# A streaming encoder layer on one core: where x's squares are summed, what TensorE does while x loads, and when three tensors are fetched

## The chip, the cores and the metric

The kernel runs on one core of one Trainium2 chip. The core has TensorE (PE, matrix products; its weight loads are listed as PEld), VectorE (DVE), ScalarE (ACT), GpSimd (POOL) and SyncE (SP, which here only issues DMAs). The metric is the device time of one execution in microseconds; lower is better. All data are fp32. A product of full precision is made of three fp32r products, of operands that were split into a high and a low part.

## What is computed

One layer for 512 prompt tokens and 128 sample tokens (640 in all, width 1024):

```python
x = x + 0.5 * swiglu(rms_norm(x, norm_ffn1_g), ffn1_w_in, ffn1_w_out)      # width 2816
h = rms_norm(x, norm_mix_g)
x = x + (g_ret * (retention(h) @ w_br_ret) + g_fox * (attention(h) @ w_br_fox)) @ w_out
x = x + 0.5 * swiglu(rms_norm(x, norm_ffn2_g), ffn2_w_in, ffn2_w_out)
x = x + (p @ w_ple) * sigmoid(rms_norm(x, norm_ple_g) @ w_ple_gate)        # p: the embedding, width 256
```

`rms_norm` divides each token by the root of the mean of its squares and multiplies by a gain for each of the 1024 channels. The mixer's states and caches are outputs too.

## The kernel before, in words

x is kept transposed: 8 chunks of 128 channels, each 128 x 640 tokens. The gain is multiplied in when a chunk is split into its high part (ACT) and low part (DVE). The divisor of each token is a factor of a product's columns, so the products can start before it is known; it is `rb` (broadcast over the partitions) or `rtok` (by token).

**The start.** SP issues x in four groups of 256 channels, and between them the weights of the first two of 22 units of 128 channels of the first feed-forward (`first_raw`). In `x_in(q)` PE transposes the group's chunks, DVE and ACT copy them out of PSUM (L644, L645), and they are split (L348 and L340 on ACT, L349 and L341 on DVE). `plain[0].products(ops, j)` multiplies the group by unit 0's weights, which `split_w` has split (L269 ACT, L270 DVE) in pieces of four chunks. `x_out(q)` writes the chunk to DRAM and calls `add_square`: ACT squares it (L511), and PE sums the squares of each token by products with a column of ones (L513, into a PSUM bank `sizes`). After the last group `token_root` works out the inverse roots in ten small DVE steps (L326 to L333), copies them to `rtok` (L518), `row_stats` broadcasts them by PE, ACT copies them out (L529), and `act` can scale unit 0's result (L546 on DVE, `Silu` L547 on ACT, L548). Three units are computed so (`Plain`). Eight 2 KB PSUM banks are shared: six named `pa`, two named `pg`. `plain[0]` holds four of `pa`, so only the first half of `plain[1]` can run before L546.

**The units after.** From unit 3 (f = 3) on, a unit is a `Seven`: seven products in place of eight, of sums of quarters of the weights (three sums in `first`, L403 to L405) and sums of x's parts (`sums`, L357 to L361, split by L291 and L292). `ffn` runs the units in groups of 8, 8 and 6, and after each group a projection adds to x's chunks, which SP fetches from DRAM and, but for the last group of the second feed-forward, writes back. In that last projection `done` is `to_ple`, which hands each chunk to the third norm.

**The second feed-forward's start.** Unit 0's weights are loaded during the mixer's last product (`begun`); then the last two quarters of the embedding's product (`w_ple`) are computed in `pg` banks and written to DRAM (`ple`, L1431), and `ffn` loads unit 1's weights (`up_raw`, L535). Two buffers hold raw weights.

**The last stage.** For each quarter q of the channels and each token block t, PE multiplies by the gate's weights, `out(t)` fetches the embedding's rows from `ple`, takes the sigmoid (L1637), multiplies (L1638), adds x, transposed back by PE (L1642), and writes the result (L1643).

**Order.** A planner gives each engine an order from a simulated timeline, and each engine keeps to its order, DMA issues on SP included. `after` and `load` add edges to that order: `load(out, in, lead)` keeps a DMA behind a PE instruction some microseconds earlier, so that no buffer is taken too soon. `blk` has 38 buffers of 128 x 640, `att` and `tmp` have 8 each.

Of the kernel before, what the change touches and what calls it, by code (L numbers as in the profile page):

```python
# [19 lines left out]
P = 128  # L20
# [111 lines left out]
def kernel(  # L132
# [101 lines left out]

    def load_gains(n0, gs):
        rows = tmp([P, P])[:len(gs) * KC, :]
        for n, g in enumerate(gs):
            nc.scalar.dma_start(rows[n * KC:(n + 1) * KC, :], g[0].rearrange("(c p) -> c p", p=P))
        gb, at = bank("pg"), slice(n0, n0 + len(gs))
        transpose(gb[:, :len(gs) * KC], rows)  # L240
        nc.vector.tensor_copy(gains[:, at].rearrange("p n c -> p (n c)"), gb[:, :len(gs) * KC])
        nc.vector.tensor_scalar(less[:, at], gains[:, at], -1.0, None, op0=ALU.mult)

    load_gains(0, (norm_ffn1_g,))


# [104 lines left out]

    def sums(ops, x0, x1, g0, g1, less, later=None):


        b12, d13, d24 = tmp(), att(shape=(P, 2, H2)), att(shape=(P, 2, H2))
        x21, x22 = (x1[:, sl] for sl in HALVES)
        nc.scalar.activation(b12, x0[:, H2:], AF.Copy, scale=g0)  # L357
        nc.vector.scalar_tensor_tensor(d13[:, 0, :], x0[:, :H2], g0, b12, op0=ALU.mult, op1=ALU.subtract)
        nc.vector.scalar_tensor_tensor(d24[:, 0, :], x22, g1, d13[:, 0, :], op0=ALU.mult, op1=ALU.add)
        nc.vector.scalar_tensor_tensor(d13[:, 1, :], x22, less, b12, op0=ALU.mult, op1=ALU.add)  # L360
        nc.vector.scalar_tensor_tensor(d24[:, 1, :], x21, g1, d24[:, 0, :], op0=ALU.mult, op1=ALU.subtract)  # L361
        if later:
# [27 lines left out]
    class Seven:  # L390
# [7 lines left out]

        def first(self, spare=False):

            a11, a12, a21, a22 = self.given
            self.as_is = Parts().add(a11, spare), Parts().add(a22, spare)
            nc.vector.tensor_tensor(a11, a21, a11, op=ALU.add)  # L403
            nc.vector.tensor_tensor(a21, a21, a22, op=ALU.add)
            nc.vector.tensor_tensor(a22, a11, a22, op=ALU.add)  # L405
            return self
# [51 lines left out]
    class Norm:  # L458
# [22 lines left out]

        def add_sums(self, c, x0, x1, later=None):
            sums(self.ops, x0, x1, self.gain(c), self.gain(c + 1), less[:, self.n, c + 1:c + 2], later)

# [22 lines left out]

        def add_square(self, ps, xc, first, last):

            sq = att(shape=(P, T))  # L510
            nc.scalar.activation(sq, xc, AF.Square)  # L511
            for t in range(TB):
                mm(ps[:, t:t + 1], sq[:, t * P:(t + 1) * P], ones[:, 0:1], first and t == 0, last, skip_group_check=True)  # L513

        def token_root(self, ps):
            rt = rsqrt_mean(ps[:, :TB], TB, 1.0 / D)
            self.rtok = const.tile([P, TB], F32, name=nm("rtok"))
            nc.vector.tensor_copy(self.rtok, rt)  # L518

# [17 lines left out]

    def ffn(xd, norm, w_in, w_o, done, ahead=None, begun=None):
        pair0 = 0
        for npair in F_GROUPS:  # L540
# [19 lines left out]
            for f in fs:  # L560
# [16 lines left out]
                if f != fs[-1]:  # L577
                    q = Seven(*quarters(up_raw(w_in, f + 1))).split()
                while waiting and f > 0:
# [37 lines left out]

    def first_raw(f, u):
        cols = slice(u * DFF + f * P, u * DFF + (f + 1) * P)
        nc.sync.dma_start(raws[f][:, 8 * u:8 * u + 8, :], w_in[:, cols].rearrange("(c p) n -> p c n", p=P))  # L620

    with tc.manual_schedule(engines={mybir.EngineType.SP}):
        for q in range(KC // 2):
            cols = slice(q * 256, (q + 1) * 256)
            xi = big((P, TB, 256))
            nc.sync.dma_start(xi[:, :4, :], x_prompt[0, :, cols].rearrange("(t p) d -> p t d", p=P))
            nc.sync.dma_start(xi[:, 4, :], x_sample.rearrange("b l d -> (b l) d")[:, cols])
            xins.append(xi)
            if q < 2:
                first_raw(0, q)  # L630
        first_raw(1, 0)
        first_raw(1, 1)
        nc.sync.dma_start(sm[:, P:], c_small[:, P:])
    norm1 = Norm(0)
    xs0 = []
    sizes = bank("pg")

    def x_in(q):
        for c in (2 * q, 2 * q + 1):
            xc = blk()  # L640
            b, b2 = bank(), bank("pg")
            for t in range(TB):
                transpose(b[:, t * P:(t + 1) * P] if t < 4 else b2[:, :P], xins[q][:, t, c % 2 * P:(c % 2 + 1) * P])
            nc.vector.tensor_copy(xc[:, :S], b)  # L644
            nc.scalar.copy(xc[:, S:], b2[:, :P])  # L645
            xs0.append(xc)
            norm1.add_parts(c, xc)
            if c % 2 == 0:
                first_parts(norm1.ops, xc[:, H2:], norm1.gain(c), "b12")

    def x_out(q):
        for c in (2 * q, 2 * q + 1):
            nc.sync.dma_start(xd[0][c], xs0[c])
            norm1.add_square(sizes, xs0[c], c == 0, c == KC - 1)

    plain = [Plain(raws[0])]
    for j in range(KC // 2):
        x_in(j)
        plain[0].products(norm1.ops, j)
        if j:  # L660
            x_out(j - 1)
        if j == 2:
            load_gains(1, (norm_mix_g, norm_ffn2_g, norm_ple_g))
    x_out(3)
    norm1.token_root(sizes)
    b0, b1 = bank("pg"), bank("pg")
    norm1.row_stats([b0, b1[:, :P]])

    def step(n):
        def run(act):  # L670
# [4 lines left out]
            for j in ((0, 1), (2, 3), ())[n]:  # L675
                norm1.add_sums(2 * j, xs0[2 * j], xs0[2 * j + 1])
            act(plain[n])
# [937 lines left out]

    x = []

    def to_ple(xc):
        x.append(xc)
        norm3.add(xc)  # L1620
        norm3.square(xc)

    ffn(xd[1], norm2, ffn2_w_in[0], ffn2_w_out[0], to_ple, begun=begun)

# [3 lines left out]
    for q in range(4):  # L1628
# [59 lines left out]
```

## Time and profile before

| | before |
|---|---|
| three runs | 1669.32, 1670.46, 1672.25 us; median 1670.46 |
| the profiled execution | 1668.46 us |
| its span, first to last instruction | 1666.4 us |
| PE busy | 1648.0 us (99%) |
| DVE, ACT busy | 1172.2 us (70%), 743.6 us (45%) |
| DMA | 248.67 MB, mean 149 GB/s |

The span is the stretch that the trace covers; the device time adds some 2 us around it. A matmul's record is longer than its share of PE's time, since records overlap; the pace is read from the starts, or from the chain of waits, whose pieces do not overlap. An fp32 matmul leaves two records.

### The profile page before, as it was taken

What the parts mean: (1) busy time and instruction counts of PE and PEld (TensorE: products, weight loads), DVE (VectorE), ACT (ScalarE), POOL (GpSimd) and SP (SyncE); (2) the same over time, 40 slices, a digit from 0 to 9 for tenths busy, and PEclk for the clock granted to TensorE, in tenths of its full rate; (3) what the DMA queues carried; (4) which work ended last, traced back from release to release, by engine and by line L of the source; (5) the groups of instructions that cost most, each with busy time, mean ns of one, the idle gap of its engine ahead of it and who ended that gap; (6) DMA issues with size and microseconds to landing.
All of it is one profiled execution on the core that took longest, in us unless ns stands there. A gap on an engine that the chain in (4) does not pass through costs nothing.

```text
span 1666.4 us, 30484 instructions
## 1 busy us (share of the span) xinstructions
PE 1648.0 (99%) x12073; PEld 1575.3 (95%) x12073; DVE 1172.2 (70%) x2524; ACT 743.6 (45%) x1506; POOL 1.4 (0%) x6
## 2 busy tenths in 40 slices
PE   8999999999999999999999999999999999999998
PEld 7999999999999888888789888999999999999998
DVE  5985687577787746667688876657885688568663
ACT  5652354244455545444434455435653355235432
POOL 0000000000000000000000000000000000000000
PEclk9999999999999999999999999999999999999999
DMA  7144324433533234576775687634324423432332
GB/s 242 52 133 140 108 78 139 146 94 106 176 111 109 70 115 148 218 259 243 284 235 168 219 272 260 228 108 146 105 78 171 132 77 120 145 116 87 122 125 87
DMA packets 228303, 248.67 MB, mean 149 GB/s; under 512 B 15264, under 2 KB 195392, under 8 KB 224064
## 3 DMA queue, kind: packets, MB, share of 16 engines
q1 hardware_dynamic: 227952, 246.64, 45.5%
q8 instruction: 95, 1.56, 0.4%
q14 instruction: 48, 0.39, 0.1%
q10 hardware_dynamic: 208, 0.08, 0.0%
HBM read 198.04 MB, written 48.65 MB: 148 GB/s over the span
## 4 chain that ended last, share of the span: by engine, by line
PE 96%; DMA 3%; DVE 1%; ACT 0%; issue 0%; SPq 0%; DVEq 0%; ACTq 0%
PE pa L205 73%; PE pg L205 19%; PE pa L228 4%; DMA raw<-in_ffn_w_in_dram 1%; DMA kv<-zdram 1%; DMA out_dram<-kv 0%; DMA zdram<-blk 0%; DMA tmp<-ple 0%; PE pg L228 0%; ACT wh L269 0%; DVE wl L270 0%; DVE tmp L1642 0%; ACT tmp L1637 0%; DVE kv L1397 0%; DVE tmp L1638 0%
## 5 line engine op out<-in xcount | busy, mean ns | idle before, releaser
L269 ACT CAST wh<-raw 128x512 fp32r<-128x512 f32 (+1 forms) x525 | 316.0, 613 | 489.8 <-PE pa L205 291.8
L205 PE MATMUL pa<-blk,wh 128*128 128x320 f32 x2344 | 512.2, 311 | 3.8 <-ACT blk L348 1.2
L270 DVE TENSOR_TENSOR wl<-raw,wh 128x512 fp32r<-128x512 f32 (+1 forms) x525 | 351.4, 678 | 93.3 <-ACT wh L269 88.3
L205 PEld LDWEIGHTS pa<-blk,wh 128*128 128x128 f32 x2344 | 388.0, 189 | 11.9 <-issue 2.8
L205 PE MATMUL pa<-blk,wl 128*128 128x320 f32 x1172 | 343.9, 309 | 0.0
L205 PE MATMUL pa<-kv,wh 128*128 128x320 f32 x1344 | 251.4, 308 | 0.0
L205 PEld LDWEIGHTS pa<-blk,wl 128*128 128x128 f32 x1172 | 216.0, 188 | 0.0
L205 PEld LDWEIGHTS pa<-kv,wh 128*128 128x128 f32 x1344 | 210.7, 188 | 0.0
L205 PE MATMUL pg<-blk,wh 128*128 128x320 f32 x768 | 176.8, 316 | 2.0 <-DVE blk L788 1.9
L205 PE MATMUL pa<-blk,blk 128*128 128x320 f32 (+2 forms) x1064 | 167.1, 304 | 0.0
L205 PE MATMUL pa<-kv,wl 128*128 128x320 f32 x672 | 155.2, 308 | 0.0
L205 PE MATMUL pg<-wh,blk 128*128 128x256 f32 x784 | 152.9, 289 | 1.6 <-ACT tmp L1430 1.6
L205 PEld LDWEIGHTS pa<-blk,blk 128*128 128x128 f32 (+1 forms) x1064 | 151.4, 183 | 2.0 <-PE pa L205 1.2
L205 PEld LDWEIGHTS pg<-blk,wh 128*128 128x128 f32 x768 | 127.5, 188 | 8.8 <-issue 4.5
L205 PEld LDWEIGHTS pg<-wh,blk 128*128 128x128 f32 x784 | 123.4, 189 | 6.2 <-issue 3.0
L205 PE MATMUL pg<-blk,wl 128*128 128x320 f32 x384 | 118.9, 310 | 0.0
L205 PE MATMUL pg<-wl,blk 128*128 128x256 f32 x392 | 112.9, 289 | 0.0
L205 PEld LDWEIGHTS pa<-kv,wl 128*128 128x128 f32 x672 | 112.8, 188 | 0.0
L270 DVE TENSOR_TENSOR blk<-raw,blk 128x512 fp32r<-128x512 f32 x82 | 56.4, 688 | 54.7 <-ACT blk L269 33.6
L269 ACT CAST blk<-raw 128x512 fp32r<-128x512 f32 x82 | 50.6, 621 | 80.1 <-DMA raw<-in_ffn_w_in_dram 63.3
L205 PE MATMUL pa<-wh,blk 128*128 128x256 f32 (+1 forms) x416 | 78.9, 285 | 0.0
L205 PEld LDWEIGHTS pg<-wl,blk 128*128 128x128 f32 x392 | 73.9, 189 | 2.5 <-issue 1.7
(260 smaller groups left out, 2175.1 us busy)
## 6 DMA issues: line engine op xcount, KB each, us to landing
raw<-in_ffn_w_in_dram SPq DMA_DIRECT2D x88, 512.0 KB, 5.2
raw<-in_w_in_mix_dram SPq DMA_DIRECT2D x25, 1024.0 KB, 5.7
raw<-in_ffn_w_out_dram SPq DMA_DIRECT2D x16, 1024.0 KB, 5.2
kv<-in_cache_fox_k_dram SPq DMA_DIRECT2D x16, 1024.0 KB, 7.0
kv<-in_cache_fox_v_dram SPq DMA_DIRECT2D x16, 1024.0 KB, 8.4
xd<-blk SPq DMA_DIRECT2D x48, 320.0 KB, 2.6
blk<-xd SPq DMA_DIRECT2D x48, 320.0 KB, 5.4
zdram<-blk SPq DMA_DIRECT2D x32, 320.0 KB, 2.8
```

The lines of the kernel that those rows point to most:

```text
L205: i = nc.tensor.matmul(out, lhsT, rhs, start=start, stop=stop, **kw)
L228: tick(nc.tensor.transpose(out, in_, ident[: in_.shape[0], : in_.shape[0]]), 0.11)
L269: nc.scalar.copy(hi, src)
L270: nc.vector.tensor_tensor(lo, src, hi, op=ALU.subtract)
```

## The change

x's squares are summed over channels on ACT, from the rows of x as they were loaded (tokens on partitions): one `Square` with a sum for each token block and group, 20 in all, then one DVE reduction; the products with ones and the bank `sizes` go. Each square is placed behind a PE instruction, and the `sums` of x's parts are placed behind the root. PE gets nine 128 x 128 fp32 matmuls of ones before x is there, and two on the first chunk. The gains' rows are loaded at the start, into `att` buffers. The first group of x and unit 0's first half of weights are loaded in two pieces each. In each `Seven` after another, the first sum of the weights is placed behind the three sums of the unit ahead. Unit 1 of the second feed-forward is loaded before the embedding's last products, which alternate between `pa` and `pg` banks. The rows of `ple` are fetched in the last projection, three loads for each quarter, into `blk` buffers, in place of 20 loads in the last stage.

```diff
+    def keep_busy(times, x=None):
+        for _ in range(times):
+            nc.tensor.matmul(busy[:, :P], ones, ones if x is None else x[:, :P], start=True, stop=True)
+
+    keep_busy(9)
+    flip_gains(0, 1, load_gains((norm_ffn1_g,)))
+    more = load_gains((norm_mix_g, norm_ffn2_g, norm_ple_g))
...
-    def sums(ops, x0, x1, g0, g1, less, later=None):
+    def sums(ops, x0, x1, g0, g1, less, later=None, behind=None):
...
-        nc.scalar.activation(b12, x0[:, H2:], AF.Copy, scale=g0)
+        i = nc.scalar.activation(b12, x0[:, H2:], AF.Copy, scale=g0)
+        if behind:
+            after(i, behind, "the tokens' sizes go first")
...
-        def first(self, spare=False):
+        def first(self, spare=False, behind=None):
...
-            nc.vector.tensor_tensor(a11, a21, a11, op=ALU.add)
+            i = nc.vector.tensor_tensor(a11, a21, a11, op=ALU.add)
+            if behind:
+                after(i, behind, "the sums of the block ahead go first")
...
-        def add_square(self, ps, xc, first, last):
-            sq = att(shape=(P, T))
-            nc.scalar.activation(sq, xc, AF.Square)
+        def add_square(self, rows, behind):
+            if not self.squares:
+                self.by_rows = tiny(KC // 2 * TB)
             for t in range(TB):
-                mm(ps[:, t:t + 1], sq[:, t * P:(t + 1) * P], ones[:, 0:1], first and t == 0, last, skip_group_check=True)
+                at, sq = len(self.squares) * TB + t, tmp([P, 256])
+                i = nc.scalar.activation(sq, rows[:, t, :], AF.Square, accum_out=self.by_rows[:, at:at + 1])
+                after(i, behind, "the parts of x go first")
+            self.squares.append(rows)
+
+        def row_root(self):
+            total = tiny(TB)
+            nc.vector.tensor_reduce(total, self.by_rows[:, :len(self.squares) * TB].rearrange("p (q t) -> p t q", t=TB), axis=AX.X, op=ALU.add)
+            self.token_root(total)
...
                 if f != fs[-1]:
-                    q = Seven(*quarters(up_raw(w_in, f + 1))).split()
+                    ahead_of = q
+                    q = Seven(*quarters(second if second is not None else up_raw(w_in, f + 1)))
+                    q.first(True, ahead_of.summed).split()
+                    second = None
...
-            nc.sync.dma_start(xi[:, :4, :], x_prompt[0, :, cols].rearrange("(t p) d -> p t d", p=P))
-            nc.sync.dma_start(xi[:, 4, :], x_sample.rearrange("b l d -> (b l) d")[:, cols])
+            n = P if q == 0 else 256
+            for lo in range(0, 256, n):
+                nc.sync.dma_start(xi[:, :4, lo:lo + n], x_prompt[0, :, q * 256 + lo:q * 256 + lo + n].rearrange("(t p) d -> p t d", p=P))
+                if lo == 0:
+                    nc.sync.dma_start(xi[:, 4, :], x_sample.rearrange("b l d -> (b l) d")[:, cols])
+                if q == 0:
+                    first_raw(0, 0, 2 if lo else 0, KC if lo else 2)
             xins.append(xi)
-            if q < 2:
-                first_raw(0, q)
+            if q == 1:
+                first_raw(0, 1)
...
+            if c == 0:
+                keep_busy(2, xc)
...
-            norm1.add_square(sizes, xs0[c], c == 0, c == KC - 1)
+        norm1.add_square(xins[q], marks[max(q - 1, 0)])
...
         plain[0].products(norm1.ops, j)
+        marks.append(issued[-1][1])
...
-            load_gains(1, (norm_mix_g, norm_ffn2_g, norm_ple_g))
+            flip_gains(1, 3, more)
     x_out(3)
-    norm1.token_root(sizes)
+    norm1.row_root()
...
-                norm1.add_sums(2 * j, xs0[2 * j], xs0[2 * j + 1])
+                norm1.add_sums(2 * j, xs0[2 * j], xs0[2 * j + 1], behind=norm1.rooted)
...
+    second = up_raw(ffn2_w_in[0], 1)
     for q in range(2):
         for t in range(TB):
-            ps = bank("pg")
+            ps = bank("pa" if t % 2 else "pg")
...
     def to_ple(xc):
+        if len(x) % 2 == 0:
+            q, three = len(x) // 2, [blk([P, 2, 256]) for _ in range(3)]
+            for i, e in enumerate(three):
+                n = min(2, TB - 2 * i)
+                load(e[:, :n, :], ple[q, :, 2 * i:2 * i + n, :], 2.0)
+            embedding.append([three[t // 2][:, t % 2, :] for t in range(TB)])
...
-            pl, g = tmp([P, 256]), tmp([P, 256])
-            load(pl, ple[q, :, t, :])
+            g = tmp([P, 256])
             nc.scalar.activation(g, pss[t][:, :256], AF.Sigmoid, scale=norm3.rtok[:, t:t + 1])
-            nc.vector.tensor_tensor(g, g, pl, op=ALU.mult)
+            nc.vector.tensor_tensor(g, g, embedding[q][t], op=ALU.mult)
```

## Rows read from the trace of the kernel before

**Rows 1.** The page: the span, and each engine's busy time, share and instructions.

```profile
span 1666.4 us, 30484 instructions
PE 1648.0 (99%) x12073; PEld 1575.3 (95%) x12073; DVE 1172.2 (70%) x2524; ACT 743.6 (45%) x1506; POOL 1.4 (0%) x6
```

**Rows 2.** The waits of PE, whole span: who for whom, total, times, longest.

```profile
PE pa L228 <- DMA kv<-in_x_prompt_dram: 5.1, 1, 5.1
...
PE pg L228 <- DVE tmp L1642: 1.4, 1, 1.4
PE pa L205 <- ACT blk L348: 1.2, 1, 1.2
PE pa L205 <- DVE tmp L546: 1.0, 1, 1.0
...
PE pa L205 <- ACT wh L269: 0.8, 1, 0.8
```

**Rows 3.** The chain of waits, 0 to 52 us: start, us, what.

```profile
7.37 1.14 ACT wh L269 x2
...
9.02 0.64 PE pa L205
...
12.64 2.50 PE pa L205 x8
15.15 0.97 PE pa L228 x8
16.11 1.01 PE pg L205 x10
17.12 1.28 PE pa L205 x8
...
39.85 1.01 PE pg L205 x10
40.86 5.22 PE pa L205 x35
46.08 0.91 PE pg L205 x8
...
47.01 0.59 ACT blk L529
```

**Rows 4.** Groups of lines, 0 to 50 us: busy us, mean ns, idle before.

```profile
L205 PE MATMUL pg<-ones,att 128*128 128x1 f32 x80 | 9.7, 235 | 0.0
...
L511 ACT ACTIVATE att<-blk 128x640 f32<-128x640 f32 x8 | 5.8, 728 | 0.0
...
L358 DVE SCALAR_TENSOR_TENSOR att<-blk,gains,tmp 128x320 f32<-128x320 f32 x2 | 1.1, 543 | 0.0
```

**Rows 5.** The timeline of ACT in the mixing stage, 996 to 999 us.

```profile
997.40 0.43 ACT L1327 ACTIVATE tmp<-tmp 128x256 f32<-128x256 f32 x1
...
997.81 0.37 ACT L1430 COPY tmp<-pa 128x256 f32<-128x256 f32 x1
```

**Rows 6.** The timeline of DVE: the root's last step.

```profile
44.91 0.17 DVE L518 COPY rtok<-ty 128x5 f32<-128x5 f32 x1
```

**Rows 7.** The timeline of ACT, 66 to 70 us.

```profile
67.63 2.18 ACT L269 CAST wh<-raw 128x512 fp32r<-128x512 f32 x4 [4.20 <-DVE raw L405]
```

**Rows 8.** A stretch: busy us of PE, PEld, DVE, ACT, POOL; clock, DMA.

```profile
47.60:68.20 20.60, 20.03 (x137) 20.03 (x138) 20.18 (x38) 13.22 (x26) 0.00 (x0) 1.00 0.19 52
```

**Rows 9.** The same view, 10 to 15 us; the granted clock stands third from the end.

```profile
10.00:15.00 5.00, 4.98 (x17) 4.01 (x18) 3.01 (x5) 3.49 (x7) 0.00 (x0) 1.00 1.11 339
```

**Rows 10.** The chain of waits over the whole span.

```profile
48.17 424.45 PE pa L205 x2926
...
1172.66 4.44 DMA raw<-in_ffn_w_in_dram
...
1619.16 5.53 DMA tmp<-ple
```

**Rows 11.** The timeline of SP, 1565 us to the end: DMA issues.

```profile
1596.07 19.55 SPq L214 DMA_DIRECT2D tmp<-ple  x6
```

More of the change, by code (lines that the diff above doesn't have):

```diff
@@ L233, with load_gains, flip_gains @@
     less = const.tile([P, 4, KC], F32, name="less")
-    def load_gains(n0, gs):
-        rows = tmp([P, P])[:len(gs) * KC, :]
+    def load_gains(gs):
+        rows = att(shape=(P, P))[:len(gs) * KC, :]
         for n, g in enumerate(gs):
             nc.scalar.dma_start(rows[n * KC:(n + 1) * KC, :], g[0].rearrange("(c p) -> c p", p=P))
-        gb, at = bank("pg"), slice(n0, n0 + len(gs))
-        transpose(gb[:, :len(gs) * KC], rows)
-        nc.vector.tensor_copy(gains[:, at].rearrange("p n c -> p (n c)"), gb[:, :len(gs) * KC])
-        nc.vector.tensor_scalar(less[:, at], gains[:, at], -1.0, None, op0=ALU.mult)
-    load_gains(0, (norm_ffn1_g,))
+        return rows
+    def flip_gains(n0, n, rows):
+        gb, at = bank("pg"), slice(n0, n0 + n)
+        transpose(gb[:, :n * KC], rows)
+        nc.vector.tensor_copy(gains[:, at].rearrange("p n c -> p (n c)"), gb[:, :n * KC])
+        nc.vector.tensor_scalar(less[:, at], gains[:, at], -1.0, None, op0=ALU.mult)
+    busy = bank("pg")
+    def keep_busy(times, x=None):
[4 more added lines that the diff above has]
+    more = load_gains((norm_mix_g, norm_ffn2_g, norm_ple_g))
     def raw_unit(src, kc, n):
@@ L397, in __init__ @@
             self.given, self.w, self.banks = (a11, a12, a21, a22), [], {}
-        def first(self, spare=False):
+        def first(self, spare=False, behind=None):
             a11, a12, a21, a22 = self.given
             self.as_is = Parts().add(a11, spare), Parts().add(a22, spare)
-            nc.vector.tensor_tensor(a11, a21, a11, op=ALU.add)
+            i = nc.vector.tensor_tensor(a11, a21, a11, op=ALU.add)
+            if behind:
+                after(i, behind, "the sums of the block ahead go first")
             nc.vector.tensor_tensor(a21, a21, a22, op=ALU.add)
-            nc.vector.tensor_tensor(a22, a11, a22, op=ALU.add)
+            self.summed = nc.vector.tensor_tensor(a22, a11, a22, op=ALU.add).ins.name
             return self
@@ L480, in add_parts, with add_sums @@
                 first_parts(self.ops, xc[:, :H2], self.gain(c), "b11")
-        def add_sums(self, c, x0, x1, later=None):
-            sums(self.ops, x0, x1, self.gain(c), self.gain(c + 1), less[:, self.n, c + 1:c + 2], later)
+        def add_sums(self, c, x0, x1, later=None, behind=None):
+            sums(self.ops, x0, x1, self.gain(c), self.gain(c + 1), less[:, self.n, c + 1:c + 2], later, behind)
         def add_pair(self, x0, x1):
@@ L517, in token_root @@
             self.rtok = const.tile([P, TB], F32, name=nm("rtok"))
-            nc.vector.tensor_copy(self.rtok, rt)
+            self.rooted = nc.vector.tensor_copy(self.rtok, rt).ins.name
         def row_stats(self, dsts):
@@ L536, in up_raw, with ffn @@
         return r
-    def ffn(xd, norm, w_in, w_o, done, ahead=None, begun=None):
+    def ffn(xd, norm, w_in, w_o, done, ahead=None, begun=None, second=None):
         pair0 = 0
@@ L616, with first_raw @@
     raws = [raw_tile()[:, :16 * P].rearrange("p (c n) -> p c n", c=16) for _ in range(2)]
-    def first_raw(f, u):
+    def first_raw(f, u, lo=0, hi=KC):
         cols = slice(u * DFF + f * P, u * DFF + (f + 1) * P)
-        nc.sync.dma_start(raws[f][:, 8 * u:8 * u + 8, :], w_in[:, cols].rearrange("(c p) n -> p c n", p=P))
+        nc.sync.dma_start(raws[f][:, 8 * u + lo:8 * u + hi, :], w_in[lo * P:hi * P, cols].rearrange("(c p) n -> p c n", p=P))
     with tc.manual_schedule(engines={mybir.EngineType.SP}):
@@ L635 @@
     xs0 = []
-    sizes = bank("pg")
     def x_in(q):
@@ L653, in x_out @@
             nc.sync.dma_start(xd[0][c], xs0[c])
-            norm1.add_square(sizes, xs0[c], c == 0, c == KC - 1)
-    plain = [Plain(raws[0])]
+        norm1.add_square(xins[q], marks[max(q - 1, 0)])
+    plain, marks = [Plain(raws[0])], []
     for j in range(KC // 2):
@@ L1614 @@
     norm3 = Norm(3)
-    x = []
+    x, embedding = [], []
     def to_ple(xc):
+        if len(x) % 2 == 0:
[4 more added lines that the diff above has]
+            embedding.append([three[t // 2][:, t % 2, :] for t in range(TB)])
         x.append(xc)
@@ L1621, in to_ple @@
         norm3.square(xc)
-    ffn(xd[1], norm2, ffn2_w_in[0], ffn2_w_out[0], to_ple, begun=begun)
+    ffn(xd[1], norm2, ffn2_w_in[0], ffn2_w_out[0], to_ple, begun=begun, second=second)
     xs = norm3.xs
```

## The prediction, made before the change was run

> **What bounds the kernel now.** The page comes first: TensorE (PE) is busy 1648.0 of 1666.4 us, every other engine has room [rows 1]. So a microsecond counts only if PE stops executing something or stops waiting. The waits of PE come next: 5.1 us for the first piece of x, 1.2 us for ACT's first scaled part (L348), 1.0 us for DVE at L546, 0.8 us for an ACT cast at the start of the second feed-forward, 1.4 us for DVE at L1642 in the last stage [rows 2]; the rest lie in the mixing stage and inside the second feed-forward, which the change leaves alone. Then the chain of waits over the first 52 us [rows 3]. The reader is to see three things in it.
>
> First, the weights' cast ends the wait for data at 7.37, and the first product starts at 9.02. Second, the same 128x320 product is slow at first: 8 take 2.50 us from 12.64 (0.31 us each), 8 take 1.28 us from 17.12 (0.16 us each). [...] PE had done only transposes, then nothing, before 9.02, and products with gaps after it. Third, from 16.11 to 40.86 the chain holds 14 pieces of `pg L205`, from 1.01 to 0.12 us, in sum 7.45 us (first and last in [rows 3]): the products with ones that sum x's squares, 80 records in the groups of lines [rows 4].
>
> After 40.86 the chain runs through PE doing the first half of `plain[1]` while DVE works out the root, up to L518 at 44.91 [rows 6], 4.2 us with that step. Then `row_stats` at 46.08, ACT's copy at 47.01, DVE's L546, and PE goes on at 48.17. From there the chain stays on PE for 424.45 us [rows 10], so what is gained by the 48th microsecond is kept, if DVE follows: DVE is busy 20.18 of the 20.60 us from 47.60 to 68.20 [rows 8], and ACT's cast for the first `Seven` unit (f = 3) at 67.63 had waited 4.20 us for DVE's L405 [rows 7]. PE reaches f = 3 at about 48.17 + 144 x 0.149 = 69.6 (48 products of `plain[1]`, 96 of `plain[2]`, at 5.22/35 us). The weight is ready at about 68.3. So DVE is there with some 1 us to spare.
>
> **Squares on ACT.** PE loses 40 matmuls (80 records): 7.45 us off the chain. ACT loses 8 squares, 5.8 us [rows 4], and gets 20 of 128x256 with a sum. The nearest row is L1327, of the same shape and kind: it starts at 997.40, and the next instruction at 997.81 [rows 5], so 0.41 us each, 8.2 us in all; ACT pays 2.4 us more, and has that room if the squares fall into its gaps. Squares of group 3 may begin when `products(2)` are done. With the terms below PE finishes `plain[1]`'s first half near 37; 72 products (10.7 us) earlier is 26. Add 5 x 0.41, one reduction, and the root: 4.2 us as now [rows 3, 6], about half of that if no casts lie between its steps. `rtok` is ready at 31 to 33. Then `row_stats` 0.91, ACT 0.59 and L546's 0.5 us, about 33 to 35 [rows 3]: before PE is out of work. So the stall that ends at 48.17 (1.2 us after 46.98) goes as well. Cover: 2 to 4 us; without it PE waits.
>
> **Sums behind the root.** Their first eight DVE steps (0.543 us each by their row [rows 4], 4.3 us) now run before the root and will run after it. DVE then needs 20.6 + 4.3 = 24.9 us from the root to f = 3: 31 to 33 becomes 56 to 58. PE gets there at 37.8 + 21.5 = 59. Cost 0, cover 1 to 3 us, at most 4.3 us if it is used up. The other order put on DVE, the three sums of one `Seven` behind those of the unit ahead, is taken at 0: PE has no wait there now.
>
> **Products of ones while x loads.** Nine fp32 matmuls need only `ones`, which the first instruction of DVE sets. `row_stats` prices them: 0.114 us a record, two records each, double at the low level: 9 x 0.46 = 4.1 us, inside the 5.1 us wait [rows 2]. The two on x's first chunk lie inside the 1.2 us wait. Cost 0; an overrun of a few tenths is hidden too, since the first product waits for the weight. Gain: from 9.02 to 15.15 the chain did 16 products, worth 2.6 us at the high level, and a few transposes, about 1 us (8 take 0.97). At most 2.5 us can come back; not all, because the second half of the weights and x's next piece are still on their way. I take 1.5 and keep 0 to 2.5.
>
> [...]
>
> **Finer first loads.** Transposes of chunk 0 can start after half the bytes of x. But the first weight cast takes four chunks, and the pieces cut it after two, so it still waits for the same bytes, and SP issues two loads more. What remains is that ACT can do L348 before the casts: 9.02 becomes 8 at best, 9.3 if the extra issues delay the weight. 0.2 us gained; ends +1.1 and -0.3.
>
> **f = 1 of the second feed-forward loaded earlier.** Now its load is issued at 1172.66, behind writes of the embedding on SP, and is 4.44 us of the chain [rows 10]; ACT stands on it, and PE waits 0.8 us [rows 2]. Ahead of those writes it has the room left by the embedding weight's cast. Gain 0.8 (0 to 0.8); next late is nothing in that row. Alternate PSUM banks there: 0, no wait of PE is recorded.
>
> **Embedding fetched in the last projection.** The chain's `tmp<-ple` at 1619.16 lasts 5.53 us [rows 10] and ends in PE's wait of 1.4 us. 20 loads become 12 on SP, earlier. They lie behind PE work if they get their `blk` places. Gain 1.4 (0 to 1.4).
>
> **Sum.** 7.45 + 1.2 + 1.5 + 0.2 = 10.35 at the start, 0.8, 1.4: 12.55. The profiled execution took 1668.46 (span 1666.4), 2.0 below the median of the three runs, 1670.46. Against its own time the sum gives 1655.9; with the same 2.0, a median of 1657.9. The best ends (2.5, 1.1) give 1656.0, and an end for PE's small waits that this change doesn't name, some 2 us, 1653.5 or so.
>
> **The rivals.**
> *Root late, chance 0.15.* ACT keeps order: suppose parts and casts push the last square to 37. Then the root is ready near 41, L546 ends near 43.5 (4.7 us gained), and DVE's 24.9 us end near 66 (3.7 us gained at f = 3). 3.7 + 2.2 gives 1664.6. For it: ACT is in order and gets 2.4 us more. Against: over the span it is busy only 45% [rows 1], and the squares need nothing but x.
> *Clock not raised, chance 0.13.* The change does not do what it says there: the low pace lasts until 15 us as now [rows 3]; 12.55 - 1.5 = 11.05 gained, 1659.4. For it: the products thin out again while data arrive. Against: PE is then at work from 1 us on and not from 5. [...]
> *Root no earlier, sums behind it, chance 0.07.* If `rtok` came at 44.9 as now, 24.9 us end at 69.8, as now: the PE time freed turns into waits. Only the two late stalls are gained, at most 2.2 us: 1668 to 1671, no change.
> *Slower, chance 0.05.* The last projection. SP is in order, and today it stands 19.55 us on six `tmp<-ple` loads until `tmp` comes free [rows 11], with nothing urgent behind. The twelve new loads stand ahead of loads of x's chunks. Their places: 8 chunks + 16 parts + 1 + 12 = 37 of 38 `blk`. If a load stands like that, PE runs on for some two chunks (2 x 36 x 0.149 = 10.7 us) and then loses about 9 us. From the second such stand it outweighs the rest: 1657.9 + 18 = 1676. Against: the places of the second norm's operands come free just before.
>
> **How the numbers follow.** The forecast, 1658, has chance 0.60. Range 1653.5 to 1666: from the best ends to a little beyond the late root; it leaves out the last two rivals, 0.12, and a little of the edges. About 0.2% (3.3 us) can be told from no change: faster 0.60 + 0.15 + 0.13 = 0.88, same 0.07, slower 0.05.
>
> **What would show it.** No `pg<-ones,att` records and 20 squares with a sum on ACT; products at 0.15 to 0.16 us each from the first one at 8 to 9 us; L518 near 31 to 33, L546 near 35 to 38, PE without a wait of a microsecond between; f = 3 near 58 to 59; no wait of PE near 1178 and 1625 (less the shift). Wrong would be: a wait of PE before L546 or f = 3 of several us, the low pace until 15 us, or PE waiting in the last projection.

## The result, and the profile after

The changed kernel takes 1659.23 us (median of 5 runs, 1658.28 to 1662.72), the kernel before 1670.46 in the same comparison: a ratio of 0.993, 95% interval 0.9911 to 0.9949, so 11.2 us or 0.7% faster, clear of the noise. The prediction was 1658.0, range 1653.5 to 1666.0. The profiled execution took 1658.28 us with a span of 1656.5, 9.9 less than the 1666.4 of before. The total came out near the forecast; several of its terms did not.

The page's first lines answer [rows 1], and the list of PE's waits (in total, times, longest) answers [rows 2]:

```profile
span 1656.5 us, 30379 instructions
PE 1643.2 (99%) x12015; PEld 1571.3 (95%) x12015; DVE 1173.6 (71%) x2525; ACT 747.4 (45%) x1538; POOL 1.4 (0%) x6
```

```profile
PE pa L205 <- ACT wh L282: 2.6, 2, 2.2
PE pg L205 <- ACT tmp L1465: 2.3, 2, 1.7
PE pg L205 <- DVE pg L817: 1.3, 1, 1.3
PE pg L205 <- DVE blk L823: 1.1, 1, 1.1
```

The first wait of 5.1 us for x and the waits before L546, at the start of the second feed-forward (0.8) and in the last stage (1.4) are gone. New is 2.2 us for an ACT cast: it lies at the start, behind the products of ones. L282 and L283 are now the casts of the weights, L531 the squares, L353 and L361 ACT's parts of x, L571 `act`.

The chain of waits over the first 62 us answers [rows 3]:

```profile
0.74 3.41 DMA kv<-in_x_prompt_dram
...
5.71 7.35 DMA raw<-in_ffn_w_in_dram
...
13.08 1.14 ACT wh L282 x2
14.22 2.61 ACT tmp L531 x13
...
16.84 0.99 ACT tmp L531 x5
17.83 0.92 ACT blk L361 x2
...
19.30 1.03 ACT wh L282 x2
20.34 0.74 ACT blk L353
...
21.12 0.86 PE pa L205 x4
...
38.65 20.55 PE pa L205 x141
```

Before, the chain stood on PE from 9.02 to 46.98. Now it stands on DMAs and their issues until 13.08, on ACT until 21.12, and the squares make up 4.1 us of ACT's 8.0 (2.61, 0.99 and a piece of 0.51 that is not shown). After that PE runs without a gap to 61.08. (Idle times of PE are counted from the ends of records, which overlap, so a wait of 0.34 us before 61.42 is what is left after 61.08.)

Where the 9.9 us came from, by the start of the same work in both traces (f = 3 is the first unit of seven products; the mixing stage begins with a step of 66 records in PE's chain, at 472.62 before and 464.94 after):

| stretch | before | after | saved |
|---|---|---|---|
| start to the first products of f = 3 | 69.22 | 61.42 | 7.80 |
| f = 3 to the mixing stage's first products | 403.40 | 403.52 | -0.12 |
| mixing stage, to the attention's output products | 633.37 | 634.72 | -1.35 |
| to the embedding's last products (`w_ple`) | 56.14 | 56.14 | 0 |
| `w_ple` and the second feed-forward | 436.13 | 433.93 | 2.20 |
| last stage, its products | 63.71 | 62.43 | 1.28 |
| the rest | 4.43 | 4.34 | 0.09 |

### The profile page after: what moved, and what is told of

It is laid out like the page before. It is cut to its first block, busy times and chain, and to the rows that moved or that the text cites. A ratio compares the mean times of both kernels' runs of the same rounds, so it can differ in the third digit from the quotient of the medians.

```text
span 1656.5 us, 30379 instructions
## 1 busy us (share of the span) xinstructions
PE 1643.2 (99%) x12015; PEld 1571.3 (95%) x12015; DVE 1173.6 (71%) x2525; ACT 747.4 (45%) x1538; POOL 1.4 (0%) x6
## 4 chain that ended last, share of the span: by engine, by line
PE 96%; DMA 2%; ACT 1%; DVE 1%; issue 0%; SPq 0%; DVEq 0%; ACTq 0%
PE pa L205 74%; PE pg L205 18%; PE pa L228 4%; DMA kv<-zdram 1%; DMA raw<-in_ffn_w_in_dram 0%; DMA blk<-foxd 0%; DMA out_dram<-kv 0%; PE pg L228 0%; ACT tmp L531 0%; ACT wh L282 0%; DMA kv<-in_x_prompt_dram 0%; DVE wl L283 0%; SPq L214 0%; DVE blk L305 0%; ACT L1484 0%
## 5 line engine op out<-in xcount | busy, mean ns | idle before, releaser
L282 ACT CAST wh<-raw 128x512 fp32r<-128x512 f32 (+1 forms) x525 | 316.9, 615 | 489.7 <-PE pa L205 302.2
L283 DVE TENSOR_TENSOR wl<-raw,wh 128x512 fp32r<-128x512 f32 (+1 forms) x525 | 352.4, 681 | 97.9 <-ACT wh L282 92.9
L283 DVE TENSOR_TENSOR blk<-raw,blk 128x512 fp32r<-128x512 f32 x82 | 56.4, 690 | 43.7 <-ACT blk L282 29.0
L205 PE MATMUL pa<-wh,blk 128*128 128x256 f32 (+1 forms) x432 | 82.8, 285 | 0.0
L282 ACT CAST blk<-raw 128x512 fp32r<-128x512 f32 x82 | 50.8, 623 | 67.1 <-DMA raw<-in_ffn_w_in_dram 51.1
```

The lines of the kernel that those rows point to most:

```text
L205: i = nc.tensor.matmul(out, lhsT, rhs, start=start, stop=stop, **kw)
L282: nc.scalar.copy(hi, src)
L283: nc.vector.tensor_tensor(lo, src, hi, op=ALU.subtract)
```

## Experiments

Unless said otherwise an edit is made to the changed kernel. Single executions differ by several us in the mixing stage alone (below), so single runs are read by stretches and not by their totals.

### Does the clock of the first products matter?

PE's start after the change (start, duration, instruction, idle time before it and what ended it), and then a table by stretches (from and to, length, busy time of PE, PEld, DVE, ACT and POOL; the granted clock is the third number from the end):

```profile
1.05 4.21 PE L253 MATMUL pg<-ones 128*128 128x128 f32 x18 [1.05 <-DVE ones L225]
...
7.19 0.65 PE L253 MATMUL pg<-blk,ones 128*128 128x128 f32 x4
10.08 1.43 PE L205 MATMUL pa<-blk,wh 128*128 128x320 f32 x4 [2.24 <-ACT wh L282]
```

```profile
8.00:10.00 2.00, 0.00 (x0) 0.00 (x0) 0.76 (x2) 0.86 (x4) 0.00 (x0) 0.84 1.05 334
10.00:13.00 3.00, 2.92 (x11) 2.88 (x12) 2.14 (x3) 1.55 (x4) 0.00 (x0) 0.50 1.12 324
13.00:16.00 3.00, 3.00 (x14) 2.88 (x13) 1.29 (x2) 2.92 (x11) 0.00 (x0) 0.50 1.11 337
16.00:20.00 4.00, 4.00 (x32) 3.97 (x31) 2.46 (x5) 4.00 (x17) 0.00 (x0) 0.98 1.14 314
```

The high pace had come (four records of ones in 0.65 us, where the first 18 took 4.21), then PE stood idle 2.24 us, and the granted clock fell to 0.50 until 16; four products took 1.43 us at 10.08. (The low and the high level of the prediction are these paces: 0.31 and 0.16 us for one 128x320 product [rows 3].) Before the change the trace has its first record of the clock at 15.21, and the column reads 1.00 ahead of it too, where products go at the low pace [rows 9, 3]; after the change the first record comes at 5.93. So with the ones the high pace came some 9 us earlier, and then it was lost again. Two runs, one without the ones and one with more of them:

```diff
-    keep_busy(9)
+    keep_busy(0)
...
-                keep_busy(2, xc)
+                keep_busy(0, xc)
```

> The change without its 11 products of ones; all else is kept. Theory (the low pace of the first products comes from what PE does just before them): in the changed kernel PE stands idle from 7.84 to 10.08 us after the ones, the granted clock there is 0.84 and then 0.50 from 10 to 16 us, and the products take 0.31 us each. So the ones have bought nothing: without them the low pace lasts as long, the first norm's sizes are ready within 0.3 us of 34.22, and the point 472 us moves by less than 0.5 us. Rival (the ones did raise the clock earlier than before, only not early enough): without them the high pace comes later than 16 us, and the same point is 1 us or more later.

```diff
-                keep_busy(2, xc)
+                keep_busy(14, xc)
```

> The change with 14 instead of 2 products of ones behind x's first chunk, to fill the idle stretch of 7.84 to 10.08 us; each took 0.25 to 0.3 us there (its two records), so 12 more fill about 3 us. Theory (the idle stretch is what lets the clock fall): the granted clock stays at 1.00 from 8 to 16 us, the products take 0.15 to 0.16 us each from the first one at about 10.2 to 10.5, and everything after is about 2 us earlier (between 1.5 and 2.5). Rival (the clock falls whatever the ones do, as products with gaps between them follow): 0.31 us each until about 16 us as in the changed kernel, and the point 472 us is where it was or up to 0.5 us later.

Without the ones the low pace lasted as long (four products in 1.42 us at 12.82, in 0.76 at 16.89), f = 3 began at 62.07 (0.65 later than after the change) and the 66-product step stood at 465.68 against 464.94. With 14, the granted clock did stay at 1.00 from 8 to 20 us, and four of the same products took 0.85 us instead of 1.43. Yet f = 3 began at 61.85. Neither moved time as its theory said. PE's start in the run with 14:

```profile
10.38 0.85 PE L205 MATMUL pa<-blk,wh 128*128 128x320 f32 x4 [0.34 <-ACT wh L282]
...
19.19 1.02 PE L205 MATMUL pa<-blk,wh 128*128 128x320 f32 x4 [1.27 <-ACT blk L361]
```

PE was faster and gave all of it back as idle time, 2.4 us in four waits between 10 and 20. What fixes f = 3 is seen when it is set against ACT's cast of the second half of unit 0's weights, which starts when that half has landed:

| run | that cast | f = 3 | difference | granted clock, 8 to 20 us |
|---|---|---|---|---|
| after the change | 13.08 | 61.42 | 48.34 | 0.72 |
| no ones | 13.75 | 62.07 | 48.32 | 1.00 |
| 14 ones | 13.37 | 61.85 | 48.48 | 1.00 |
| whole loads (below) | 11.34 | 59.81 | 48.47 | 1.00 |
| whole loads, timed | 11.64 | 60.12 | 48.48 | 1.00 |
| whole loads, no ones | 12.60 | 61.13 | 48.53 | 1.00 |

(The column reads 1.00 in the runs without ones too, though four of their products took 1.42 us at 12.82 and 1.44 at 13.27; see the last section.) So 48.3 to 48.5 us pass from there to f = 3 at either pace of PE (four products in 1.43 or 0.85 us), and the ones, kept or dropped, move this by less than 0.1 us. Two more runs with the changed kernel's start, below, give 48.32 each; other orders on DVE and ACT, also below, give 47.8 to 50.2. The 0.65 us of the first run are a landing that was 0.67 us later.

### Is it the squares on ACT?

In the run with 14 products of ones, the squares of the first two groups are put behind the second group's products:

```diff
-        norm1.add_square(xins[q], marks[max(q - 1, 0)])
+        norm1.add_square(xins[q], marks[max(q - 1, 1)])
```

> The run with 14 products of ones behind x's first chunk, with one more edit: ScalarE's squares of x's first two groups wait for the products of the second group instead of the first. Theory (with the clock high, ScalarE is what binds from 13 to 21 us: in the run with 14 products of ones the chain of waits passes through ten squares from 14.51 to 18.58 while TensorE stands 1.27 us for the part of chunk 2 that is queued behind them): the part of chunk 2 is ready near 15.5, TensorE's idle time between 10 and 21 us falls from 2.4 us to under 1, the products that began at 21.57 begin 1.5 to 3 us earlier, and the first feed-forward ends (the 66-product step that was at 465.50) 1 to 2.5 us earlier; less if the root, now later, is needed first. Rival (the data of x or of the weights bind there, and ScalarE only fills the time): the products at 21.57 and the step at 465.50 stay within 0.4 us.

The part of chunk 2 came early as expected, and PE had no wait there. But a wait of 1.84 us stood 8 us later, again for a part that is queued behind squares:

```profile
27.06 1.48 PE L205 MATMUL pa<-blk,wh 128*128 128x320 f32 x6 [1.84 <-ACT blk L353]
```

f = 3 began at 62.35, 0.5 later than with 14 ones alone. Neither theory as written held: this order moved the wait, and while the squares stood back ACT itself was idle for 1.42 us (for a chunk's copy) and 0.68 us (for a weight), which it is not in the run with 14 ones. That ACT binds by its sum of work up to x's last parts, whatever the order, is argued from this and not shown. A run further below takes work out of that stretch; it needs the next result first.

### Finer first loads

```diff
-            n = P if q == 0 else 256
-            for lo in range(0, 256, n):
...
+            nc.sync.dma_start(xi[:, :4, :], x_prompt[0, :, cols].rearrange("(t p) d -> p t d", p=P))
+            nc.sync.dma_start(xi[:, 4, :], x_sample.rearrange("b l d -> (b l) d")[:, cols])
...
-            if q == 1:
-                first_raw(0, 1)
+            if q < 2:
+                first_raw(0, q)
```

> The change with x's first piece and the weight's first piece loaded whole, as in the kernel before; the rest is kept. Theory (the finer pieces hold the weight up: SP stood from 2.72 to 4.16 us ahead of the second part of the weight, until the first part of x had landed): the first cast of the weight starts near 7.4 instead of 9.41, the first product near 9.0 instead of 10.1, and the idle stretch of PE shrinks; all that follows comes 1.0 to 1.3 us earlier, some 2 us if the clock no longer falls in the shorter idle stretch. Rival (the bytes themselves take that long, however they are cut): the first cast within 0.4 us of 9.41 and no gain.

SP's issues with the finer pieces (after the change) and the chain of the run with whole loads:

```profile
1.78 0.43 SPq L648 DMA_DIRECT2D raw<-in_ffn_w_in_dram  x1
2.25 0.47 SPq L656 DMA_DIRECT2D kv<-in_x_prompt_dram  x1
4.16 0.37 SPq L648 DMA_DIRECT2D raw<-in_ffn_w_in_dram  x1
...
5.71 0.43 SPq L648 DMA_DIRECT2D raw<-in_ffn_w_in_dram  x1
```

```profile
0.73 4.54 DMA kv<-in_x_prompt_dram
...
5.29 0.34 SPq L655
...
5.67 5.64 DMA raw<-in_ffn_w_in_dram
...
11.34 1.14 ACT wh L282 x2
```

SP issues four loads, and the fifth goes out only when the first has landed (4.15 with the small piece, 5.27 whole); after the change it waits 1.4 us for that landing, SP's only wait for a load in the first 12 us. Why the fifth waits is not shown. With the finer pieces the fifth is the rest of the first half of the weights: the first cast is at 9.41 instead of 7.47. The second half is issued at about the same time, 5.71 and 5.67, but then lands at 13.06 instead of 11.31. f = 3 began 1.61 us earlier than after the change. The theory held; the pieces cost 1.3 to 1.6 us at f = 3 (the second from the run below). Over all traces the cast of the second half starts at 12.75 to 13.76 with the finer loads (nine) and at 11.34 to 12.60 with whole ones (four). Why it lands later though it is issued at the same time was not found.

The time, 1651.47, was 7 us below the changed kernel, far more than the start explains. It was timed in several executions:

> The run with whole first loads once more, timed. One look gave 1651.47, 7 us below the changed kernel, though its start is only 1.6 us earlier: 5.1 us came from the mixing stage, whose instructions stand in another order there (629.64 us from the 66-product step to the first attention-output product, against 634.72). Theory (this order, which no edit touched, is worth the 5 us): a median of 1650 to 1653.5, and 628 to 631 us for the stage again. Rival (the mixing stage varies that much from execution to execution of one order): a median of 1655 to 1658, or 632 us or more for the stage in this profile.

The median is 1651.59 (1649.86 to 1653.79), ratio to before 0.9894, interval 0.9877 to 0.991. The start is 1.30 us shorter than in the trace after the change, the mixing stage 5.88. The mixing stage of that run, and of the changed kernel (the first numbers are the stretch, its length and PE's busy time):

```profile
463.61:1092.45 628.84, 626.41 (x4973) 558.37 (x4973) 445.19 (x1102) 292.33 (x630) 0.00 (x0) 1.00 0.57 195
```

```profile
464.94:1099.66 634.72, 629.67 (x4974) 560.16 (x4973) 445.95 (x1102) 293.40 (x630) 0.00 (x0) 1.00 0.57 193
```

The waits of PE in that stage, whole loads, to be set beside the second to fourth wait of the changed kernel above:

```profile
PE pg L205 <- ACT tmp L1460: 1.4, 1, 1.4
PE pa L205 <- DVE blk L305: 0.7, 1, 0.7
PE pa L205 <- ACT tmp L1460: 0.3, 1, 0.3
```

The waits for DVE's L817 and L823 are not there, and PE is busy 3.3 us less: after the change PE stands idle for 1.75 us up to 989.82, and at 991.91 eight 128x256 products take 3.35 us (granted clock 0.83 from 990 to 1000 us). No edit touched this stage. Its instructions stand in another order in the second half of the stage; the planner makes each engine's order from a simulated timeline, and we take it that the edits at the start change that timeline. Apart from the run with the squares on PE, which has a third, two orders occur (but for two instructions of DVE in two of the runs), and their lengths do not overlap: 633.4 to 638.9 us in eight executions (before and after the change, the runs without ones, with 14, with later squares, and others), 628.8 to 630.0 in five (whole loads twice, the next two runs, and early squares).

### DVE's order

```diff
-            def act(q, ah, al):
+            def act(q, ah, al, behind=None):
...
+                    if k == len(ahead) - 1:
+                        begun = Seven(*quarters(up_raw(w_in, k + 1))).first(True)
+                    step(lambda q: act(q, ah, al, begun.summed if begun else None))
```

> The change with one order put right on DVE: the sums of the third unit of the first feed-forward (f = 3) are issued ahead of the activation products of the unit before it. Theory (PE's wait of 2.2 us at 59.2 comes from DVE's order: its products wait for PE until 59.23 with the third sum queued behind them, and DVE idles 1.0 us meanwhile): the wait falls to at most 0.4 us, and the point 472 us comes 1.8 to 2.2 us earlier. Rival (DVE is simply late there, as the eight sums moved behind the root fill it): the wait stays above 1.5 us, now for sums or casts that follow.

This rested on a misread row: the longest wait for a cast, 2.2 us, is the one at the start, and f = 3 waits only 0.34 us, first after the change, then in this run, where it is gone:

```profile
61.42 0.56 PE L205 MATMUL pa<-blk,wh 128*128 128x320 f32 x2 [0.34 <-ACT wh L282]
```

```profile
61.16 0.46 PE L205 MATMUL pa<-blk,wh 128*128 128x320 f32 x2
```

DVE's order was the cause, and it is worth 0.3 us (the wait) to 0.5 us (from the cast to f = 3, 47.82 against 48.34). The total of 1651.61 is the other order of the mixing stage (628.93).

```diff
-                norm1.add_sums(2 * j, xs0[2 * j], xs0[2 * j + 1], behind=norm1.rooted)
+                norm1.add_sums(2 * j, xs0[2 * j], xs0[2 * j + 1])
```

> The change without its rule that the first eight sums of halves (two groups of four on DVE) stand behind the root; they may go before or between its steps. Theory (the root is in time only since nothing stands between its steps): DVE puts the sums, 0.54 us each, between the root's steps; rtok comes 1 to 4 us later than 34.22, and TensorE waits for the activation products by up to 2 us, or not at all as far as it had products left to do (the f = 3 wait, 0.34 us, falls then). Rival (the rule does nothing): rtok within 0.3 us of 34.22.

```profile
41.42 0.56 PE L205 MATMUL pa<-blk,wh 128*128 128x320 f32 x2 [0.98 <-DVE tmp L571]
```

`rtok` came at 36.60, 2.4 us later, and PE waited 0.98 us; f = 3 began 49.05 us after the cast instead of 48.34. The rule is worth 0.7 us.

### The squares back on PE

```diff
-        norm1.add_square(xins[q], marks[max(q - 1, 0)])
+            norm1.add_square(sizes, xs0[c], c == 0, c == KC - 1)
...
-    norm1.row_root()
+    norm1.token_root(sizes)
```

> The change with x's squares summed on TensorE by products with ones, as in the kernel before, on whole 128x640 chunks; all else is kept. Theory (the squares' move carries nearly all of the gain of the start, 7.45 us of 80 records plus the 1.2 us stall): the end of the first feed-forward (464.94 in the changed kernel, 472.62 before) goes back to 472 to 474; above 472.62 by the 1.0 us that the finer loads cost. Rival (the other parts of the change at the start bring a share of their own): it stays below 471.

The first feed-forward ended at 479.30, not 472 to 474: the run took 1673.20 us, 3.9 more than the kernel before beside it. Two stretches (the clock is the third number from the end) and PE's waits show the rest:

```profile
10.00:16.00 6.00, 5.90 (x27) 5.53 (x26) 3.19 (x5) 2.98 (x6) 0.00 (x0) 0.51 1.11 333
16.00:22.00 6.00, 5.83 (x29) 5.55 (x28) 0.57 (x1) 1.14 (x2) 0.00 (x0) 0.64 1.09 328
```

```profile
50.79 1.38 PE L205 MATMUL pg<-sm,rtok 128*128 128x128 f32 x10 [1.23 <-DVE rtok L535]
53.95 0.57 PE L205 MATMUL pa<-blk,wh 128*128 128x320 f32 x2 [1.78 <-DVE tmp L563]
```

With PE on the chain again the low clock counts, and it lasts until 20.3; and the sums behind a root at 50.57 come too late. Without the squares' move the other edits of the start do harm, 6.7 us at the end of the first feed-forward (479.30 against 472.62). So this run does not price the move alone, and no run has it alone on the kernel before.

### The middle and the last stage

```diff
-    second = up_raw(ffn2_w_in[0], 1)
+    second = None
...
-            ps = bank("pa" if t % 2 else "pg")
+            ps = bank("pg")
```

> The change with the middle stage as before: the second feed-forward's f = 1 weight loaded when f = 0 is done, and the embedding's last products in one kind of PSUM bank. The start is the same, so only the stretch from the first of these products (1155.80 in the changed kernel) to the second norm's statistics products (1184.68; 28.88 us, against 30.62 before) is read. Theory (these two edits are worth the 1.7 us): 30.2 to 30.8 us, with a wait of TensorE of 0.7 us or more for an ACT cast of a weight or for the embedding's bank. Rival (the stretch is shorter since the order of the instructions there is another): 28.9 again.

The stretch took 30.63 us, against 28.88 after the change and 30.62 before, and the old wait is back to the hundredth:

```profile
1173.81 0.56 PE L205 MATMUL pa<-blk,wh 128*128 128x320 f32 x2 [0.76 <-ACT wh L282]
```

From the same products to the last stage it is 435.65 against 433.93, so the two edits are worth 1.7 us. They can be told apart without a run: with either choice of banks the program has the same instructions in the same order on every engine, with the same semaphores, whether the first line is there or not (as built; neither mixture was run). So the alternating banks bring the 1.7 us, the earlier issue of the load included. How the 1.7 us divide beyond the wait of 0.76 us is open.

```diff
+            pl, g = tmp([P, 256]), tmp([P, 256])
+            load(pl, ple[q, :, t, :])
...
-            nc.vector.tensor_tensor(g, g, embedding[q][t], op=ALU.mult)
+            nc.vector.tensor_tensor(g, g, pl, op=ALU.mult)
```

> The change with the embedding's rows fetched in the last stage, as in the kernel before; the rest is kept, the order of the mixing stage too. Read from the last stage alone (first product of the gate to the end of the last products: 63.71 us before, 62.43 in the changed kernel). Theory (the fetch is worth the wait of 1.4 us for DVE at the product with the embedding): 63.5 to 64.0 us with that wait back in the list of waits. Rival (another part of the change shortened this stage): 62.4 us and no such wait.

```profile
1611.77 7.31 DMA tmp<-ple
```

```profile
1619.98 0.69 PE L228 MATMUL pg<-sm,blk 128*128 128x128 f32 x2 [3.10 <-DVE tmp L1678]
```

The wait is back, larger than before (3.1 against 1.4, the load 7.31 against 5.53), and the stage took 67.17 us, not 63.5 to 64: here too the clock fell after the wait (0.84 from 1620 to 1630). The mechanism held, the size did not: in this execution the late fetch cost 4.7 us.

### Taking work off ACT, and the ones once more

Whole loads, and the first group's squares wait for no product:

```diff
-        norm1.add_square(xins[q], marks[max(q - 1, 0)])
+        norm1.add_square(xins[q], marks[q - 1] if q else None)
```

> Whole first loads, as in the run with whole loads, and the squares of x's first group wait for no product: ScalarE does these five (0.40 us each) when their data have landed, near 5.3 us, where it stood idle until 7.47 us. Theory (ScalarE's whole work between 12 and 29 us binds the start, so only work moved out of that stretch helps, not another order within it, as the run with squares later showed): ScalarE's last scaled part (it began at 27.70 in the run with whole loads) begins 1 to 2 us earlier, rtok comes 1 to 2 us before 32.62, the f = 3 products 0.7 to 1.8 us before 59.81. In all 1648 to 1652 us, since the order of the mixing stage's instructions is that of the run with whole loads. Rival (data or DVE bind): f = 3 within 0.4 us of 59.81.

A miss: 1654.10 us (1652.43 to 1655.47), f = 3 at 61.64. The squares did run from 5.08 to 7.1, but the chain now lies on PE from the second cast on:

```profile
11.42 0.63 ACT wh L282
12.09 0.90 PE pa L205 x2
...
14.70 3.20 PE pa L205 x12
```

PE had stood idle for 1.73 us (a piece of x) and 1.60 us (the cast), its pace was low until 18 us (12 products in 3.20 us, granted clock 0.69 from 10 to 21), and with ACT out of the way that counted: 50.22 us from the cast to f = 3. So ACT's work and PE's low clock are two bounds that lie within 2 us of each other; taking work off one shows the other. Both together (early squares and a clock that stays up) were not tried.

Whole loads without the ones:

> Whole first loads and no products of ones. In the runs so far the f = 3 products begin 51.2 to 51.5 us after the first product where the finer loads stand (with 18, 42 or no records of ones before it, granted clock 0.50 to 1.00), and 50.5 and 50.7 us after it with whole loads. Theory (the clock of the first products is hidden behind ScalarE's work, the ones are worth nothing): 50.3 to 51.0 us again, and f = 3 within 0.6 us of 59.8 to 60.1. Rival (with data in time the ones matter): 51.5 us or more. The order of the mixing stage's instructions is here that of the kernel before and of the changed kernel; if it is worth 5 us, as the runs with the other order showed (628.8 to 630.0 us against 633.4 to 638.9), the stage takes 633 us or more and the median lies 3 to 7 us above the 1651.59 of the run with whole loads, though the start is as early.

f = 3 began at 61.13, 52.1 us after the first product. By the yardstick on record, the first product, the rival won; but that yardstick was the wrong one. The second half of the weights landed 1.0 to 1.3 us later than in the two runs with whole loads, and from its cast to f = 3 it is 48.53 us, as ever:

```profile
5.60 6.97 DMA raw<-in_ffn_w_in_dram
12.60 0.63 ACT wh L282
13.27 1.44 PE pa L205 x4
```

Here the chain stands on PE at the low pace from the cast on, and not on ACT's squares, and it comes to the same 48.5 us: without the idle stretches of early squares the two bounds lie within tenths of a microsecond. (So they do in the run with the middle stage as before: PE has the chain until 19.32, at the low clock until 16.56, and it is 48.32.)

Why the half landed later (6.97 us from issue, against 5.64 and 6.16 with ones) is open; each is one execution. The mixing stage took 635.93 us, in the order of before, as expected. The median is 1658.89 (ratio 0.9929, interval 0.9911 to 0.9946), 7.3 us above whole loads with ones, a little more than the 3 to 7 expected. Of the 9.6 us between the two profiled spans (1658.7 and 1649.1) the mixing stage has 7.1 and the way to f = 3 1.0: two kernels that differ by eleven matmuls are parted mostly by an order that these matmuls have nothing to do with.

## Why the prediction was right, and where not

**Squares on ACT, 7.45 + 1.2: right in size.** From the second cast to f = 3 it was 57.01 us before (69.22 - 12.21) and is 48.34: 8.67 saved, 8.65 predicted. The two rows of the kernel before, and `rtok` after the change:

```profile
12.21 1.12 ACT L269 CAST wh<-raw 128x512 fp32r<-128x512 f32 x2
...
69.22 0.46 PE L205 MATMUL pa<-blk,wh 128*128 128x320 f32 x2
```

```profile
34.22 0.17 DVE L543 COPY rtok<-ty 128x5 f32<-128x5 f32 x1
```

That the two agree so closely is luck in part: before, this cast was not on the chain, which stood on PE from 9.02. The last group's squares began at 26.09 (26 predicted), but the root took 6.1 us and not 4.2, with parts of x and a weight's cast between its steps, so `rtok` came at 34.22 (31 to 33 predicted). PE had work until 37.37, so this cost nothing, and the stall before `act` went. But "ACT has that room if the squares fall into its gaps" failed: ACT has no gap from 13 to 30 us (busy 16.89 of 17.00), and squares stand in the chain. Their price was paid by the clock term.

**Clock, 1.5: wrong.** As in the second rival the low pace lasted until 16: the first record of the clock, at 5.93, is 1.00, and it fell to 0.50 at 9.3, in the idle 2.24 us. That work of PE ahead of the first products raises their pace was the author's assumption; four of them took 0.85 us with 14 ones and 1.44 without. But the low pace was not why the gain was missing. The step that failed is the step from a faster TensorE to an earlier f = 3: with the clock kept up (1.00 from 8 to 20 us, 14 ones) the gain was nil as well, as ACT's queue takes as long from the cast on as PE at the low pace (48.48 and 48.34 us to f = 3). The rival's 1659.4 is close to the median by accident. With whole loads five transposes took 1.33 us at 6.34 without the ones, and four products 1.44 us at 13.27; with the ones the same five took 0.76 us at 6.24. These runs do not tell whether the ones did this by what they are or by PE being at work 4 us earlier (from 1.05, not 5.07).

**Finer loads, 0.2 gained: wrong in sign.** The cast of the second half of the weights starts 0.87 us later than before (13.08 against 12.21, where it stood behind other work of ACT and did not wait for the load) and 1.4 to 1.7 later than with whole loads and the ones; the worst end allowed was 0.3 lost. The first product came at 10.08, where 8 to 9.3 was predicted. The step that failed is "it still waits for the same bytes": SP's fifth issue waits for the first landing, and with the finer pieces the fifth is the rest of the first half of the weights.

**Start in sum:** 8.67 - 0.87 = 7.80, where 10.35 was predicted. How the 7.80 divides depends on the cast as the point of division; only the sum is measured.

**Sums behind the root, 0: nearly.** 0.34 us at f = 3 at 61.42, not 58 to 59.

**Second feed-forward, 0.8: mis-sized, and put down to the wrong line.** 2.20 gained. The 0.76 us wait went, but the earlier load, costed at 0.8, does nothing by itself; the alternating banks, costed at 0 since no wait of PE was recorded there, bring 1.7 us with that wait. The other 0.5 is there with both lines undone too (435.65 against 436.13) and was not traced. **Embedding, 1.4: right**, 1.28, and in the one run that undoes it the late fetch cost 4.7.

**The mixing stage, taken as left alone,** lost 1.35 us in this execution with the same order, and swings by 5.6 us between executions of that order. The sum of 12.55 was 2.65 too high against the profiled span (9.9 saved) and 1.3 against the medians. So the closeness of the total is luck in part: 2.55 too much at the start and 1.35 lost in the mixing stage stand against 1.40 more from the second feed-forward.

## What to carry to other kernels

When a step is taken off the bounding engine, follow the chain through the engine that receives it: here ACT's queue became the bound and swallowed what a faster TensorE would have given. A wait that an edit takes away need not be that edit's work: undo each line by itself. A load cut into pieces is also one more issue, and what stands behind it in the queue pays: here 1.3 to 1.6 us at f = 3. Where a planner sets the order, a small edit may move instructions far away: compare the orders and single stretches before a total is put down to the edit; the best kernel of this study (whole loads, the rest of the change kept, 1651.59 us) owes to such an order 5.9 of the 7.4 us by which its profiled span is shorter than the changed kernel's (1649.1 against 1656.5).

## What the hardware showed unexpectedly

- A granted clock of 1.00 does not prove the high pace at the start: without ones it reads 1.00 from 8 to 20 us while four products took 1.44 us at 10.77, against 0.85 at 10.38 with 14 ones. The column reads 1.00 ahead of the first record of the clock, which came at 15.2 us before the change and at 5.9 after it.
- The same start does not keep the same clock: in three other runs with the changed kernel's start PE stood idle for 2.7 to 3.0 us, the first products after that still ran at the high pace (0.85 us for four), and the clock fell to 0.50 only near 12 us; after the change it fell at 9.3 and in a fourth such run at 9.7, after 2.24 and 2.81 us. The length of the idle stretch alone does not decide; what does was not found.
- The time from issue to landing of the second half of unit 0's weights lay at 5.6 to 7.0 us with whole loads and at 7.3 to 7.9 with the finer ones (6.8 with the squares on PE). Where nothing behind it was changed, f = 3 moved with its landing one for one.
